# One softmax left undivided, an operand moved to ScalarE, conditioning sums kept out of one projection's end, one weight split queued behind a norm

## The chip, the cores and the metric

The kernel runs on one NeuronCore of a Trainium2 chip. A core has five engines, each working through its own list of instructions in order: TensorE (PE, matrix products), VectorE (DVE), ScalarE (ACT), GpSimd (POOL) and SyncE (SP, which here issues nearly all the DMAs). They wait for each other through semaphores. The metric is the device time of one execution in microseconds. The kernel before takes 2352.55 us, the median of three runs (2351.01 to 2356.51). A difference under about 0.2%, 4.7 us, can't be told from none.

## The reference

Two decoder layers over 256 tokens of width 2048, all in float32. Cut to what matters here:

```
c_act = silu(c)
for l in range(2):
    sh_a, sc_a, g_a, sh_m, sc_m, g_m = split(c_act @ w_ada[l] + b_ada[l])
    h = x * (1 + sc_a) + sh_a
    fq, fk, fv, ff, dq, dk, dv = split(h @ w_in[l])
    # 8 "fox" heads: a causal softmax with a decay added to the logits
    p = softmax(fq @ fk.T * 128**-0.5 + fcum_q - fcum_k)      # fcum = cumsum(log_sigmoid(ff + b_f))
    fox_o = p @ fv
    # 8 differential heads: two causal softmax maps, 64 wide each
    a = softmax(dq0 @ dk0.T / 8) - lam * softmax(dq1 @ dk1.T / 8)
    diff_o = a @ dv
    diff_o = diff_o * rsqrt(mean(diff_o**2) + 1e-5) * subln_g * (1 - lam_init)
    y = concat(fox_o, diff_o) @ w_o[l]
    x = layernorm(alpha * x + (1 + g_a) * y)
    h = x * (1 + sc_m) + sh_m
    x = layernorm(alpha * x + (1 + g_m) * (relu(h @ w_up[l])**2 @ w_down[l]))
```

## The kernel before

**Weights in two parts.** Each weight block (256 rows by 512 columns, 512 KB) is loaded by SyncE into one of seven buffers `raw`. `split_w` (L128) makes two float32r parts of it: ScalarE copies it to the high part `wh` (L135), VectorE subtracts that from it and gets the low part `wl` (L136). The activations have a high and a low part too, and each product is three matmuls: high by high, high by low, low by high (L302 to L304, and the transposed forms L328 to L331). `block` (L279) is the step that every projection loop takes: it runs what is due beside the loop, then loads and splits one block. Three blocks can be split ahead of TensorE.

**Conditioning sums beside it.** The product with `w_ada` has one row only and is done on VectorE: for each vector, 16 blocks of 512 KB are loaded (`rawa`, in the same seven buffers) and added up, scaled by one number per partition, into `acc` (the first of a sum is L147, the others L149). `side_step` (L250) takes such pieces at a rate per block, `RATES`, with one row per layer: in the mixer a rate for the first part, one for the heads, one for the output projection, then those of the MLP. If a sum is needed and not ready, `side_until` takes all its pieces at once. A finished sum is turned by eight TensorE transposes (L166) and reduced (L171, L173).

**Heads.** While the projections run, the heads are spawned as tasks whose steps come due a given number of blocks later. A differential head computes four logit tiles (two maps, two query tiles), and per map and query tile `softmax_rows` (L606): VectorE adds the mask and takes the row minimum (L612), ScalarE takes the exponential with the row sum `su` (L614), VectorE the reciprocal (L616). The second map is scaled by minus lambda over its sum (L671 on VectorE, L672 on ScalarE), and one VectorE operation divides the first map and adds the second (L674). TensorE turns the result (L622 to L624), multiplies it with the values (L681 to L683), and the output is normalized by its mean square (L687 to L692). A fox head divides its map on ScalarE (L644). Its decay comes from a matmul whose operand `FR` is one VectorE product (L877) per four heads.

**The stretch between two sub-layers.** A projection that ends a sub-layer has `proj_tail` (L349): its last blocks (four in the mixer) are all loaded first, then all their matmuls are made for query tile 0 and after that for tile 1. So tile 0 can go on while TensorE still works for tile 1: VectorE multiplies the product with the gate, adds it to the residual and takes statistics (L510 to L513), aggregates them (L517, L519), GpSimd makes one over the standard deviation (L521), and VectorE normalizes the tile in four pieces of 512 columns (L526). Tile 1 follows in the same way, piece by piece. TensorE turns the pieces (L485), ScalarE scales and shifts them by the conditioning (L498), and VectorE makes the high part of the new `hT` (L500) and the low part (L501). Then the next projection starts. There are three such stretches: after layer 0's mixer (the first norm below), after layer 0's MLP (the second) and after layer 1's mixer (the third).

**What sets the order.** The kernel is written with a layer that records the operations and lists them per engine by its own estimate of when each could run. What two operations share decides what may not be turned round; the rest can change place with any edit. `tc.issue_after(ins)` asks that the operations recorded inside it come behind `ins` on its engine.

## Time and profile before

| | |
|---|---|
| median of three runs | 2352.55 us |
| profiled execution, its own time | 2351.68 us |
| its span, first to last instruction | 2350.0 us |
| TensorE busy | 2273.3 us, 97% |
| TensorE weight loads busy | 1937.6 us, 82% |
| VectorE busy | 1801.3 us, 77% |
| ScalarE busy | 1157.2 us, 49% |
| mean granted TensorE clock | 0.995 |

The busy shares are averages over the whole span. TensorE is busy in all but a few places, so the reader looks for the places where it stood idle, and for what ended each of those waits. A timeline row gives start, duration, engine, line, operation and tiles, and in brackets the idle time of the engine just before it with what ended that time. Rows that show "x4" are several instructions of one kind merged.

### The profile page before, as it was taken

The numbers are of one execution on the slowest core, as the hardware profiler recorded it, in microseconds if no ns is written. First come the engines' busy times: TensorE is split into PE (matmuls) and PEld (weight loads), VectorE is DVE, ScalarE is ACT, GpSimd is POOL, SyncE is SP. The second block draws the span as 40 slices with busy tenths as digits, with TensorE's granted clock in tenths as the row PEclk, the third lists the DMA queues.
The fourth block names the chain that finished last, engine by engine and source line by source line (L and its number), as shares of the span: only waits on it lengthen the run. The fifth ranks groups of instructions, "written<-read, shape, count | busy, mean of one in ns | idle before, by whom it ended". The sixth has DMA issues, their size and how long they took to land.

```text
span 2350.0 us, 32557 instructions
## 1 busy us (share of the span) xinstructions
PE 2273.3 (97%) x12060; PEld 1937.6 (82%) x12060; DVE 1801.3 (77%) x2363; ACT 1157.2 (49%) x1696; POOL 35.2 (1%) x60
## 2 busy tenths in 40 slices
PE   4999999899999999999999999999999999999998
PEld 3878788699989888888877778888888888888886
DVE  7899989989888778888777976767675666555657
ACT  3543675345546346346444664544644643643542
POOL 0000010000000000000000000000000000000000
PEclk9999999999999999999999999999999999999999
DMA  9998678888898889888758877764687677755553
GB/s 346 330 331 308 207 262 311 313 314 330 302 350 300 305 281 315 314 289 302 273 185 307 295 233 242 255 212 168 225 268 241 229 244 242 228 194 190 187 190 124
DMA packets 174975, 619.32 MB, mean 264 GB/s; under 512 B 20104, under 2 KB 21208, under 8 KB 174816
## 3 DMA queue, kind: packets, MB, share of 16 engines
q1 hardware_dynamic: 174816, 617.25, 76.1%
q8 instruction: 94, 1.54, 0.3%
q14 instruction: 65, 0.53, 0.1%
HBM read 615.07 MB, written 2.10 MB: 263 GB/s over the span
## 4 chain that ended last, share of the span: by engine, by line
PE 81%; DVE 8%; DMA 5%; issue 3%; ACT 2%; POOL 0%; SPq 0%; DVEq 0%; ACTq 0%; POOLq 0%
PE mm L303 14%; PE mm L302 14%; PE mm L304 14%; PE mm L938 7%; PE bank L938 7%; PE mm L940 4%; PE bank L940 4%; PE mm L344 3%; PE mm L331 3%; PE mm L330 3%; PE mm L328 3%; DVE wl L136 3%; DMA rawa<-in_w_ada_T_dram 2%; DVE acc L149 2%; PE mm L346 2%
## 5 line engine op out<-in xcount | busy, mean ns | idle before, releaser
L135 ACT CAST wh<-raw 128x1024 fp32r<-128x1024 f32 x752 | 790.1, 1051 | 932.8 <-PE mm L304 500.1
L136 DVE TENSOR_TENSOR wl<-raw,wh 128x1024 fp32r<-128x1024 f32 x752 | 915.0, 1222 | 340.6 <-ACT wh L135 338.0
L149 DVE SCALAR_TENSOR_TENSOR acc<-rawa,cact,acc 128x1024 f32<-128x1024 f32 x368 | 471.0, 1280 | 114.2 <-DMA rawa<-in_w_ada_T_dram 57.6
L303 PE MATMUL mm<-wl,Hs 128*128 128x512 f32 x992 | 386.7, 390 | 1.5 <-DVE wl L136 1.5
L302 PE MATMUL mm<-wh,Hs 128*128 128x512 f32 x992 | 386.6, 390 | 0.0
L304 PE MATMUL mm<-wh,Hs 128*128 128x512 f32 x992 | 386.5, 390 | 0.0
L938 PE MATMUL mm<-hT,wh 128*128 128x512 f32 x768 | 286.7, 396 | 0.0
L938 PE MATMUL bank<-hT,wh 128*128 128x512 f32 x768 | 286.4, 395 | 0.0
L303 PEld LDWEIGHTS mm<-wl,Hs 128*128 128x128 f32 x992 | 186.3, 188 | 40.6 <-DVE wl L136 2.3
L304 PEld LDWEIGHTS mm<-wh,Hs 128*128 128x128 f32 x992 | 186.3, 188 | 38.8
L302 PEld LDWEIGHTS mm<-wh,Hs 128*128 128x128 f32 x992 | 186.3, 188 | 38.3
L940 PE MATMUL mm<-hT,wl 128*128 128x256 f32 x768 | 215.9, 281 | 0.0
L940 PE MATMUL bank<-hT,wl 128*128 128x256 f32 x768 | 215.8, 281 | 0.0
L302 PE MATMUL mm<-wh,hT 128*128 128x512 f32 x512 | 201.4, 400 | 5.8 <-DVE hT L500 5.7
L303 PE MATMUL mm<-wl,hT 128*128 128x512 f32 x512 | 203.2, 397 | 2.4 <-DVE wl L136 2.2
L304 PE MATMUL mm<-wh,hT 128*128 128x512 f32 x512 | 200.5, 392 | 0.0
L328 PE MATMUL mm<-hT,wh 128*128 128x256 f32 x640 | 181.2, 284 | 1.1 <-DVE hT L500 1.1
L330 PE MATMUL mm<-hT,wh 128*128 128x256 f32 x640 | 181.0, 284 | 0.2 <-DVE hT L501 0.2
L331 PE MATMUL mm<-hT,wl 128*128 128x256 f32 x640 | 180.2, 285 | 0.7 <-DVE wl L136 0.3
L938 PEld LDWEIGHTS bank<-hT,wh 128*128 128x128 f32 x768 | 144.1, 188 | 33.4
L938 PEld LDWEIGHTS mm<-hT,wh 128*128 128x128 f32 x768 | 144.1, 188 | 33.3
L940 PEld LDWEIGHTS mm<-hT,wl 128*128 128x128 f32 x768 | 145.4, 189 | 0.6 <-DVE wl L136 0.3
(256 smaller groups left out, 3000.3 us busy)
## 6 DMA issues: line engine op xcount, KB each, us to landing
rawa<-in_w_ada_T_dram SPq DMA_DIRECT2D x256, 512.0 KB, 5.3
raw<-in_w_up_dram SPq DMA_DIRECT2D x256, 512.0 KB, 4.8
raw<-in_w_down_dram SPq DMA_DIRECT2D x256, 512.0 KB, 4.6
raw<-in_w_in_dram SPq DMA_DIRECT2D x192, 512.0 KB, 5.0
rawa<-in_w_ada_G_dram SPq DMA_DIRECT2D x128, 512.0 KB, 5.2
raw<-in_w_o_dram SPq DMA_DIRECT2D x64, 512.0 KB, 4.4
gb<-in_ln_g_dram SPq DMA_DIRECT2D x12, 256.0 KB, 5.8
bb<-in_ln_b_dram SPq DMA_DIRECT2D x12, 256.0 KB, 5.3
```

The source lines that it names most:

```text
L135: nc.scalar.copy(wh, raw)
L136: nc.vector.tensor_sub(wl, raw, wh.bitcast(F32))
L149: nc.vector.scalar_tensor_tensor(acc, raw, k, acc, ALU.mult, ALU.add)
L302: nc.tensor.matmul(o, lhsT=hi, rhs=wh, start=start, stop=False)
L303: nc.tensor.matmul(o, lhsT=hi, rhs=wl, start=False, stop=False)
L304: nc.tensor.matmul(o, lhsT=lo, rhs=wh, start=False, stop=stop)
L328: nc.tensor.matmul(o, lhsT=wh[:, j, cs], rhs=hT[:, kt, 0, :], start=first and kt == kt0 and f % 2 == 0, stop=False)
L330: nc.tensor.matmul(o, lhsT=wh[:, j, cs], rhs=hT[:, kt, 1, :], start=False, stop=False)
L331: nc.tensor.matmul(o, lhsT=wl[:, j, cs], rhs=hT[:, kt, 0, :], start=False, stop=last and kt == kt1 - 1 and f % 2 == 1)
L344: nc.tensor.matmul(pu[f], lhsT=wh[:, j, cs], rhs=hT[:, kt].rearrange("p a s -> p (a s)"), start=kt == 0, stop=False)
L938: nc.tensor.matmul(pu[f], lhsT=wh[:, j, cs], rhs=hT[:, kt].rearrange("p a s -> p (a s)"), start=kt == kt0, stop=False)
L940: nc.tensor.matmul(pu[f][:, 0:S], lhsT=wl[:, j, cs], rhs=hT[:, kt, 0, :], start=False, stop=kt == kt1 - 1)
```

## The change

1. `diff_head`: all four row tiles get their exponentials first (`exp_rows`). The first map is no longer divided by its sum s0. The second map is scaled by r = -lambda s0 / s1 and added to it, in one VectorE operation per query tile. The factor s0 that the output then carries goes out in the root-mean-square normalization, whose epsilon becomes epsilon times s0 squared (`es`). A fox head takes one reciprocal for both its row tiles.
2. `fr_later`: the decay's operand `FR` is made by four ScalarE operations in place of one VectorE operation.
3. `proj_tail` gets a flag `quiet`, set in layer 0's mixer: its four blocks take no pieces of conditioning sums. Layer 0's rates rise from 0.8, 0.8, 1.0 to 0.9, 0.9, 1.12.
4. `split_w`: the first low part that is made after the first piece of a norm's tile 1 is queued behind that piece.

```diff
-RATES = ((0.8, 0.8, 1.0, 0.6, 1.2), (1.1, 0.53, 0.64, 0.25))
+RATES = ((0.9, 0.9, 1.12, 0.6, 1.2), (1.1, 0.53, 0.64, 0.25))
...
         nc.scalar.copy(wh, raw)
-        nc.vector.tensor_sub(wl, raw, wh.bitcast(F32))
+        with tc.issue_after(behind[0]) if behind else nullcontext():
+            nc.vector.tensor_sub(wl, raw, wh.bitcast(F32))
+        del behind[:]
...
-    def proj_tail(po, lhs, wrows, c0, kt0, kt1, done):
+    def proj_tail(po, lhs, wrows, c0, kt0, kt1, done, quiet=False):
...
-            ws.append(block(wrows(kb, c0), 2, CW, (room[:, i, 0], room[:, i, 1]) if i < 4 else None))
+            ws.append(block(wrows(kb, c0), 2, CW, (room[:, i, 0], room[:, i, 1]) if i < 4 else None,
+                            quiet))
...
                 for t in range(1, NT):
-                    normalize(t, q, *ms[t])
+                    ins = normalize(t, q, *ms[t])
+                    if q == 0:
+                        behind[:] = [ins]
...
-        pr = []
+        su = sm.tile([P, 2, NT], F32, tag="sd", name="su", bufs=2)
+        pr, p1 = [], []
         for qt in range(NT):
-            nk = (qt + 1) * P
-            p1, r1 = softmax_rows(pss[1][:, qt, 0:nk], qt)
-            nc.vector.tensor_mul(r1, r1, neglam[:, l:l + 1])
-            nc.scalar.mul(p1, p1, r1)
-            p0, r0 = softmax_rows(pss[0][:, qt, 0:nk], qt)
-            nc.vector.scalar_tensor_tensor(p0, p0, r0, p1, ALU.mult, ALU.add)
-            pr.append(p0)
+            for cc, p in ((1, p1), (0, pr)):
+                p.append(exp_rows(pss[cc][:, qt, 0:(qt + 1) * P], qt, su[:, cc, qt:qt + 1]))
+
+        r = sm.tile([P, NT], F32, tag="r", name="r", bufs=2)
+        nc.vector.reciprocal(r, su[:, 1, :])
+        nc.vector.scalar_tensor_tensor(r, su[:, 0, :], neglam[:, l:l + 1], r, ALU.mult, ALU.mult)
+        es = sm.tile([P, NT], F32, tag="es", name="es", bufs=4)
+        nc.vector.scalar_tensor_tensor(es, su[:, 0, :], RMS_EPS, su[:, 0, :], ALU.mult, ALU.mult)
+        for qt in range(NT):
+            nc.vector.scalar_tensor_tensor(pr[qt], p1[qt], r[:, qt:qt + 1], pr[qt], ALU.mult, ALU.add)
...
-            nc.vector.tensor_mul(FR, FG.unsqueeze(1).broadcast_to([P, 4, S]),
-                                 sel[:, g * 4:g * 4 + 4].unsqueeze(2).broadcast_to([P, 4, S]))
+            for i in range(4):
+                nc.scalar.mul(FR[:, i, :], FG, sel[:, g * 4 + i:g * 4 + i + 1])
...
-                proj_tail(pos[0], lhs_o, wo, 3 * CW, 8 - OTAIL, 8, lambda t: finish(3, pos[0], t))
+                proj_tail(pos[0], lhs_o, wo, 3 * CW, 8 - OTAIL, 8, lambda t: finish(3, pos[0], t), l == 0)
```

The edits shift the lines: L136 becomes L137, L147 and L149 become L149 and L151, L500 and L501 become L504 and L505, L510 to L519 become L514 to L523, L526 becomes L530, L612 becomes L618.

VectorE at the first norm, from tile 0's last product to tile 1's first pieces. `tmp` is the product with the gate, `mv`, `ve` and `rs` the statistics, `acc` a conditioning sum. Before:

```order
L149 SCALAR_TENSOR_TENSOR acc<-rawa,cact,acc 128x1024 x2
L510 TENSOR_TENSOR tmp<-mm,gate_2_1_3702 128x512 x2
L511 TENSOR_TENSOR xacc<-xacc,tmp 128x512 x2
L513 BN_STATS stats<-xacc 128x6 x2
L517 BN_AGGR mv<-stats 128x2
L149 SCALAR_TENSOR_TENSOR acc<-rawa,cact,acc 128x1024
L519 TENSOR_SCALAR ve<-mv 128x1
L517 BN_AGGR mv<-stats 128x2
L136 TENSOR_TENSOR wl<-raw,wh 128x1024
L526 TENSOR_SCALAR xacc<-xacc,mv,rs 128x512 x4
L519 TENSOR_SCALAR ve<-mv 128x1
L136 TENSOR_TENSOR wl<-raw,wh 128x1024
```

The same place now:

```order
L530 TENSOR_SCALAR xacc<-xacc,mv,rs 128x512 x4
L149 TENSOR_SCALAR acc<-rawa,cact 128x1024
L514 TENSOR_TENSOR tmp<-mm,gate_2_1_3497 128x512
L515 TENSOR_TENSOR xacc<-xacc,tmp 128x512
L517 BN_STATS stats<-xacc 128x6
L521 BN_AGGR mv<-stats 128x2
L523 TENSOR_SCALAR ve<-mv 128x1
L530 TENSOR_SCALAR xacc<-xacc,mv,rs 128x512 x2
L137 TENSOR_TENSOR wl<-raw,wh 128x1024
L504 CAST hT<-h_4447 128x2x256
L137 TENSOR_TENSOR wl<-raw,wh 128x1024
L505 TENSOR_TENSOR hT<-h_4447,hT 128x2x256
```

Before, tiles 0 and 1 went through the steps together, with sums and low parts between them. Now tile 0 is through all its steps first, one new sum's first piece stands ahead of tile 1, and the low parts stand behind tile 1's first two pieces, the second of them between the high and the low part of `hT`.

VectorE at the third norm, from tile 1's pieces on (`h` is ScalarE's scaled piece). Before:

```order
L526 TENSOR_SCALAR xacc<-xacc,mv,rs 128x512 x4
L500 CAST hT<-h_15312 128x2x256
L501 TENSOR_TENSOR hT<-h_15312,hT 128x2x256
L500 CAST hT<-h_15322 128x2x256
L501 TENSOR_TENSOR hT<-h_15322,hT 128x2x256
```

And now:

```order
L530 TENSOR_SCALAR xacc<-xacc,mv,rs 128x512 x3
L137 TENSOR_TENSOR wl<-raw,wh 128x1024
L504 CAST hT<-h_15116 128x2x256
L137 TENSOR_TENSOR wl<-raw,wh 128x1024
L505 TENSOR_TENSOR hT<-h_15116,hT 128x2x256
L504 CAST hT<-h_15126 128x2x256
```

Three low parts that stood ahead of tile 0's steps in the list stand behind tile 1's pieces now: the first two are in these rows, the third four pairs later.

VectorE in layer 1's first differential head, from its last logit tile to its two finished rows (`s`). Before:

```order
L616 RECIPROCAL rs<-su 128x1
L149 SCALAR_TENSOR_TENSOR acc<-rawa,cact,acc 128x1024
L674 SCALAR_TENSOR_TENSOR s<-s,rs 128x128
L616 RECIPROCAL rs<-su 128x1 x2
L561 SCALAR_TENSOR_TENSOR xacc<-bb,xacc 128x512
L671 TENSOR_TENSOR rs<-rs,neglam 128x1
L136 TENSOR_TENSOR wl<-raw,wh 128x1024
L674 SCALAR_TENSOR_TENSOR s<-s,rs 128x256
```

And now:

```order
L151 SCALAR_TENSOR_TENSOR acc<-rawa,cact,acc 128x1024
L680 RECIPROCAL r<-su 128x2
L683 SCALAR_TENSOR_TENSOR es<-su 128x2
L567 SCALAR_TENSOR_TENSOR xacc<-bb,xacc 128x512
L681 SCALAR_TENSOR_TENSOR r<-su,neglam,r 128x2
L137 TENSOR_TENSOR wl<-raw,wh 128x1024
L685 SCALAR_TENSOR_TENSOR s<-s,r 128x128
L685 SCALAR_TENSOR_TENSOR s<-s,r 128x256
```

The two finished rows now come one right behind the other, both behind the low part that stood between them.

## Rows read from the trace of the kernel before

**Rows 1.** The page's first part: busy us, share of the span, instructions.

```profile
span 2350.0 us, 32557 instructions
...
PE 2273.3 (97%) x12060; PEld 1937.6 (82%) x12060; DVE 1801.3 (77%) x2363; ACT 1157.2 (49%) x1696; POOL 35.2 (1%) x60
```

**Rows 2.** TensorE's waits: line, waited for, us in total, times, longest.

```profile
PE bank L485 <- DVE xacc L526: 15.1, 4, 6.9
...
PE mm L303 <- DVE wl L136: 4.7, 7, 1.2
...
PE bank L623 <- DVE s L674: 2.1, 4, 0.9
```

**Rows 3.** Timeline of TensorE around the first norm: start, us, operation.

```profile
443.63 0.50 PE L303 MATMUL mm<-wl,MXd 128*128 128x512 f32 x1 [1.07 <-DVE wl L136]
...
459.78 0.39 PE L304 MATMUL mm<-room,MXf 128*128 128x512 f32 x1
467.02 0.66 PE L485 MATMUL bank<-ident,xacc 128*128 128x128 f32 x2 [6.86 <-DVE xacc L526]
467.48 1.92 PE L166 MATMUL bank<-ident,acc 128*128 128x128 f32 x8
470.49 3.16 PE L485 MATMUL bank<-ident,xacc 128*128 128x128 f32 x14 [1.10 <-DVE xacc L526]
...
473.72 0.37 PE L330 MATMUL mm<-hT,wh 128*128 128x256 f32 x1
```

**Rows 4.** Timeline of VectorE before and in the first norm.

```profile
423.24 0.74 DVE L147 TENSOR_SCALAR acc<-rawa,cact 128x1024 f32<-128x1024 f32 x1
...
463.37 1.21 DVE L149 SCALAR_TENSOR_TENSOR acc<-rawa,cact,acc 128x1024 f32<-128x1024 f32 x1
...
464.74 1.16 DVE L136 TENSOR_TENSOR wl<-raw,wh 128x1024 fp32r<-128x1024 f32 x1
```

**Rows 5.** Timeline of SyncE in the first norm: the next sum's loads.

```profile
464.61 1.64 SPq L156 DMA_DIRECT2D rawa<-in_w_ada_T_dram  x2
```

**Rows 6.** Timeline around the third norm, TensorE and VectorE.

```profile
1614.59 0.69 DVE L510 TENSOR_TENSOR tmp<-mm,gate 128x512 f32<-128x512 f32 x1 [3.13 <-PE mm L304]
...
1617.88 1.92 DVE L526 TENSOR_SCALAR xacc<-xacc,mv,rs 128x512 f32<-128x512 f32 x4 [0.66 <-POOL rs L521]
...
1619.60 0.39 PE L304 MATMUL mm<-room,MXf 128*128 128x512 f32 x1
...
1620.03 0.69 DVE L510 TENSOR_TENSOR tmp<-mm,gate 128x512 f32<-128x512 f32 x1 [0.23 <-PE mm L304]
...
1623.33 1.91 DVE L526 TENSOR_SCALAR xacc<-xacc,mv,rs 128x512 f32<-128x512 f32 x4 [0.67 <-POOL rs L521]
1623.93 3.27 PEld L485 LDWEIGHTS bank<-ident,xacc 128*128 128x128 f32 x16 [3.73 <-DVE xacc L526]
...
1625.92 0.43 DVE L500 CAST hT<-h 128x512 fp32r<-128x512 f32 x1 [0.68 <-ACT h L498]
1626.38 0.69 DVE L501 TENSOR_TENSOR hT<-h,hT 128x512 fp32r<-128x512 f32 x1
...
1627.19 0.48 PE L938 MATMUL mm<-hT,wh 128*128 128x512 f32 x1
```

**Rows 7.** Windows: busy us of PE, PEld, DVE, ACT, POOL; granted clock, DMA share, GB/s.

```profile
240.00:270.00 30.00, 29.12 (x152) 21.91 (x150) 29.45 (x88) 19.33 (x43) 0.00 (x0) 1.00 0.59 193
...
443.00:460.00 17.00, 16.37 (x70) 12.99 (x70) 16.73 (x18) 4.89 (x5) 0.00 (x0) 1.00 0.96 356
...
465.00:470.00 5.00, 2.37 (x10) 2.00 (x10) 4.12 (x8) 0.00 (x0) 2.76 (x2) 0.50 0.68 211
...
1205.00:1207.00 2.00, 2.00 (x8) 1.71 (x7) 1.97 (x4) 2.00 (x5) 0.00 (x0) 0.50 0.00 0
...
1627.00:1630.00 3.00, 3.00 (x19) 2.63 (x18) 2.90 (x7) 2.53 (x6) 0.00 (x0) 0.98 0.00 0
```

**Rows 8.** DMA issues of the page's last part: count, KB each, us to landing.

```profile
rawa<-in_w_ada_T_dram SPq DMA_DIRECT2D x256, 512.0 KB, 5.3
```

More of the change, by code (lines that the diff above doesn't have):

```diff
@@ L216, in decoder @@
     hold = [0]
+    behind = []
     nop = lambda: None
@@ L525, in normalize @@
         xs = xacc[:, t, q * CW:(q + 1) * CW]
-        nc.vector.tensor_scalar(xs, xs, mean, rs, ALU.subtract, ALU.mult)
+        return nc.vector.tensor_scalar(xs, xs, mean, rs, ALU.subtract, ALU.mult).ins
     def norm_first(stats):
@@ L604, in heads_T, with exp_rows @@
         return oT
-    def softmax_rows(ps, qt):
+    def exp_rows(ps, qt, su):
         nk = (qt + 1) * P
@@ L612, in softmax_rows @@
         nc.vector.tensor_tensor_reduce(s, ps, m, 1.0, 3.0e38, ALU.add, ALU.min, mn)
-        su = sm.tile([P, 1], F32, tag="su", name="su", bufs=4)
         nc.scalar.activation(s, s, AF.Exp, bias=mn, scale=-1.0, accum_out=su)
-        rs = sm.tile([P, 1], F32, tag="rs4", name="rs", bufs=4)
-        nc.vector.reciprocal(rs, su)
-        return s, rs
+        return s
     def probs_T(p0, p1):
@@ L641, in fox_head @@
                              start=False, stop=qt == NT - 1)
+        su = sm.tile([P, NT], F32, tag="su", name="su", bufs=2)
         for qt in range(NT):
-            p, rs = softmax_rows(ps[:, qt, 0:(qt + 1) * P], qt)
-            nc.scalar.mul(p, p, rs)
-            pr.append(p)
+            pr.append(exp_rows(ps[:, qt, 0:(qt + 1) * P], qt, su[:, qt:qt + 1]))
+        rs = sm.tile([P, NT], F32, tag="rs4", name="rs", bufs=2)
+        nc.vector.reciprocal(rs, su)
+        for qt, p in enumerate(pr):
+            nc.scalar.mul(p, p, rs[:, qt:qt + 1])
         yield GAP
@@ L687, in diff_head @@
             nc.scalar.activation(o[:, qt, :], po[:, qt * P:(qt + 1) * P], AF.Square, accum_out=ms[:, qt:qt + 1])
-        nc.vector.tensor_scalar(ms, ms, 1.0 / HD, RMS_EPS, ALU.mult, ALU.add)
+        nc.vector.scalar_tensor_tensor(ms, ms, 1.0 / HD, es, ALU.mult, ALU.add)
         ri = sm.tile([P, NT], F32, tag="ri", name="ri")
```

## The prediction

> **What bounds the kernel now.** I read the page's first part first. TensorE is busy for 2273.3 of 2350.0 us, VectorE for 77% of the span [rows 1]. So a gain can only come from the 77 us in which TensorE stands idle, or from work that leaves TensorE. The second view is the table of what TensorE waited for. The largest wait that the change touches is that for the normalized residual: 15.1 us in four waits, the longest 6.9 [rows 2]. The longest is in the first norm: TensorE stops at 459.78 + 0.39 = 460.17, and I call this moment T; its pieces resume at 467.02, pause once more for 1.10 us, and the first matmul that needs the low part of the new `hT` starts at 473.72 [rows 3]. From T to there it is 13.55 us. Third I read the same stretch for VectorE: at 463.37, with tile 1 waiting, it makes a piece of a conditioning sum (1.21 us), and at 464.74 a low part (1.16 us) [rows 4]. The next sum's loads are issued there too, at 464.61 [rows 5]. The third norm shows what the stretch takes when no sums stand in it [rows 6]: its last matmul ends at 1619.60 + 0.39 = 1619.99, and the same kind of matmul starts at 1627.19, after 7.20 us.
>
> All sums are against the profiled execution's own time, 2351.68 us: 0.87 below the median of the runs shown, and inside their scatter. TensorE gates everything between these places, so I count what is taken off its idle time as taken off the whole.
>
> **First norm.** Tile 0's chain now runs alone. In the third norm it takes 5.2 us (1614.59 to 1617.88 + 1.92 = 1619.80) and is through before TensorE has finished tile 1 [rows 6]; I take the same here, so it costs nothing. Tile 1's chain by the third norm's rows: from the last matmul to the first normalized piece 1623.33 - 1619.99 = 3.34 us. Two pieces of 1.91 / 4 = 0.48 us each bring T + 4.30. The first low part, 1.16 [rows 4], ends at T + 5.46. Meanwhile the transposes start 0.12 us after the first piece (1623.93 against 1623.81), so at T + 3.94, and the scaled piece reaches the CAST 1.99 us later (1625.92), at T + 5.93; it takes 0.43, to T + 6.36. The second low part ends at T + 7.52, the low part of `hT` (0.69) at T + 8.21, and the matmul starts 0.12 later (1627.19 against 1627.07), at T + 8.33 [rows 6]. That is 13.55 - 8.33 = 5.22 us saved: **-5.2**.
>
> Ahead of tile 1 stands the first piece of the next sum, of a kind that took 0.74 us at 423.24 [rows 4]. VectorE waits there for TensorE anyway (3.13 us in the third norm [rows 6]), so the piece costs nothing if its load lands early, and 0.74 if it lands just at T. If the load lands later, everything of tile 1 is queued behind it on VectorE, and TensorE behind that. It can be issued earlier than before, because the quiet blocks leave no sum pieces to wait for, but its buffer comes free only with a low part of the tail. I take 0.74, **+0.7**, with 0 below; above see the fourth rival.
>
> The eight transposes of the old sum, 1.92 us at 467.48, ran while TensorE had nothing to do [rows 3], at half clock (0.50 over 465 to 470 [rows 7]). Now the sum ends before the tail, and they stand in running work, at full clock: half of 1.92, **+1.0** (0 to 1.9).
>
> The tail loses its sums. One wait of TensorE there, 1.07 us at 443.63 for a low part [rows 3], stood where VectorE was busy for 16.73 of 17.00 us and the DMA queues for 96% [rows 7]. With the loads and pieces gone I expect most of it to go: **-0.8** (0 to -1.1).
>
> **Sums moved forward.** The pieces don't vanish; they go into layer 0's heads and projections, at 0.9 for 0.8 per block. That is a tenth of a piece of 1.21 us [rows 4] per block, some 2.5 us of VectorE over about 21 blocks of the heads. Against it go the two products `FR` and the smaller operations of the heads. VectorE was busy for 29.45 us of the 30 from 240 to 270 [rows 7], so there it hides nothing more. I take 0, with -2.5 to +2.5 as bounds, since that is the work that may be added and what TensorE's remaining L303 waits show as losable, 4.7 - 1.07 = 3.6 us, is of the same size [rows 2, 3].
>
> **Low parts behind the piece, third and second norm.** In the third norm all three low parts were finished before. Now: pieces 1 to 3 end at 1623.33 + 3 x 0.48 = 1624.77, a low part at 1625.93, the CAST at 1626.36, the second low part at 1627.52, the low part of `hT` at 1628.21, so the matmul starts at 1628.33 and not at 1627.19 [rows 6]: +1.1. What it clears, tile 0's start, lay beneath tile 1's matmuls. In the second norm TensorE's list puts other matmuls ahead of those that need the low part; I take +0.1. Together **+1.2** (0 to 2.3).
>
> **Heads.** TensorE waited four times for finished rows `s`, 2.1 us, longest 0.9 [rows 2]. Undivided, the first map needs no reciprocal, and three of four reciprocals go, with the scaling by ScalarE. But all four exponentials are awaited before the first row, and in the first head a low part now stands before both rows. I take off two thirds: **-1.4** (0 to -2.1). `FR` on ScalarE costs nothing, since that engine is busy for 49% [rows 1]; if a head's exponential comes right behind it, its four parts delay that one by about what VectorE's product took.
>
> **Clock at the restart.** In the first norm TensorE had eight more transposes right before its matmuls. After a long idle stretch the granted clock was 0.50 (1.2 of 2.4 GHz) over 1205 to 1207, with matmuls, but 0.98 over 1627 to 1630 [rows 7]. The 2.00 us of the first stretch would be 1.0 at full clock, so a slow restart loses 1.0 and a fast one nothing. The third norm is the nearer of the two, with the same transposes ahead: **+0.3** (0 to 1.0).
> The Trainium skill (TensorE: Matmul & The Clock Gate, the part on PE-mode transpose) says that a transpose doesn't count as a busy PE in the way that a matmul does. By that rule the first matmuls behind the sixteen transposes run slow, and the term would be +1.0 in place of +0.3. The third norm's row, 0.98 with only transposes ahead of it, speaks against the rule; the row at 1205 agrees with it.
>
> **The sum.** -5.2 + 0.7 + 1.0 - 0.8 + 0 + 1.2 - 1.4 + 0.3 = -4.2; 2351.7 - 4.2 = 2347.5 us. A difference under 0.2%, 4.7 us, can't be told from none: faster means below 2347.8, slower above 2357.3. The forecast stands right at the first of these.
>
> **Rivals.**
> - *The other waits of the heads go too.* VectorE gets many short operations less, and TensorE's L303 waits for low parts (3.6 us outside the tail) vanish. For it: they stand where VectorE is full [rows 7]. Against it: the higher rates fill VectorE again. -4.2 - 3.6: 2343.9.
> - *The sums bite in layer 0.* The 2.5 us of pieces all end up in front of low parts that TensorE waits for. For it: 29.45 of 30 us busy [rows 7]. Against it: projections before and after have slack. -4.2 + 2.5: 2350.0.
> - *The fresh sum's piece is somewhat late,* so half of the first norm's gain is lost: -4.2 + 2.6, 2350.1. For it: the DMA queues are 96% busy until 460 [rows 7].
> - *Slower: the fresh sum's load is issued as late as before.* At 464.61 [rows 5] plus the 5.3 us that such a load takes at the median [rows 8] it lands at 469.9, its piece ends at 470.65, T + 10.5. Tile 1 starts only then, and the matmul comes at T + 10.5 + 8.33 = T + 18.8 and not T + 13.55: +5.3 where -4.5 was counted. The sum is -4.2 + 9.8 = +5.6, 2357.3. For it: the piece stands ahead of tile 1 in VectorE's list. Against it: the tail loads no sum pieces, so SyncE is there sooner. From a landing at about T + 4.2, 464.4, on, the change is slower than before.
> - *The change does not do what it says:* no sign of it, since the three places in the order show it; it is in none of the chances.
>
> **How the numbers follow.** Forecast 0.47; the waits gone too 0.15; sums bite 0.20; piece somewhat late 0.10; load as late as before 0.08. The forecast's own range is its sum's nearer bounds, 2345.5 to 2350. The range for 8 in 10 reaches from a part of the first rival and a little beyond for the heads' bound, 2343, to 2353, the second and third with the third norm's upper bound; it leaves out most of the fourth. Faster by over 0.2%: half of the forecast (0.26), nearly all of the first rival (0.14), and 0.05 of the second, whose bound is two-sided: 0.45. Slower by over 0.2%: the fourth rival and some chance of two mishaps together, 0.09. Within: 0.46.
>
> **What would show it.** In the profile after, the row of the first norm's wait for the residual should be about 4 us in place of 6.9 and be followed by the matmul with the low part near T + 8.3; VectorE should have no sum piece but one of 0.74 us there. The eight transposes should be in front of the tail. The wait of 1.07 us in the tail should be gone. In the third norm two low parts should stand between tile 1's pieces and the low part of `hT`, and the matmul should start 8.3 us after the last one, not 7.2. Waits for `s` should be at most 0.7 us. If VectorE waits at the fresh sum's piece for a DMA past T, the fourth rival or the third holds; if the L303 waits between 240 and 300 grow, the second does; if they vanish, the first. A gain much above 8 us, or one that comes from layer 1's projections, would prove this picture wrong.

## The result and the profile after

The changed kernel takes 2365.99 us, the median of four runs (2364.45 to 2367.14), against 2353.35 for the kernel before on the same chip. The ratio is 1.0058, with a 95% interval of 1.0045 to 1.0070: it is slower by 0.6%, where 2347.5 us and a range to 2353 were forecast. The forecast was wrong. The profiled execution took 2364.45 us.

The page's first part of the changed kernel (busy us, share of the span, instructions), to be held against [rows 1]:

```profile
span 2362.7 us, 32436 instructions
...
PE 2280.1 (97%) x12060; PEld 1941.0 (82%) x12060; DVE 1791.2 (76%) x2295; ACT 1151.5 (49%) x1680; POOL 35.3 (1%) x60
```

VectorE has 10 us less to do, and yet the span is 12.7 us longer. TensorE makes the same 12060 matmuls, but is busy 6.8 us longer: that is clock, not work (the mean granted clock is 0.992 and was 0.995). The table of what TensorE waited for (line, waited for; us, times, longest), to be held against [rows 2]:

```profile
PE bank L489 <- DVE xacc L530: 10.9, 3, 3.8
...
PE mm L306 <- DVE wl L137: 11.0, 9, 2.9
...
PE mm L334 <- DVE wl L137: 2.6, 4, 1.3
...
PE bank L625 <- DVE s L685: 1.4, 2, 1.1
```

The norms' wait fell from 15.1 to 10.9 us, and that for finished rows from 2.1 to 1.4. But the wait for low parts (L306, formerly L303) rose from 4.7 to 11.0. The timeline says where. TensorE in the first norm (start, us, operation), which answers to [rows 3]:

```profile
459.06 1.04 PE L168 MATMUL bank<-ident,acc 128*128 128x128 f32 x8
...
470.63 0.40 PE L307 MATMUL mm<-room,MXf 128*128 128x512 f32 x1
475.29 2.82 PE L489 MATMUL bank<-ident,xacc 128*128 128x128 f32 x12 [3.83 <-DVE xacc L530]
...
479.50 0.39 PE L333 MATMUL mm<-hT,wh 128*128 128x256 f32 x1 [1.00 <-DVE hT L505]
```

From the last matmul, 470.63 + 0.40 = 471.03, to the matmul that needs the low part it is 8.47 us now. So the norm itself gained 5.1 us. But it begins at 471.0 and not at 460.2: the time was lost ahead of it. TensorE's two waits in the output projection, and the granted clock behind each of them and, in the last row, at the third norm (windows: us; busy us of PE, PEld, DVE, ACT, POOL; clock, DMA share, GB/s):

```profile
423.64 0.79 PE L306 MATMUL mm<-wl,MXd 128*128 128x512 f32 x1 [2.89 <-DVE wl L137]
...
449.61 0.50 PE L306 MATMUL mm<-wl,MXd 128*128 128x512 f32 x1 [2.33 <-DVE wl L137]
```

```profile
423.60:427.00 3.40, 3.36 (x8) 2.69 (x9) 3.40 (x3) 0.00 (x0) 0.00 (x0) 0.51 0.94 284
...
451.00:454.50 3.50, 3.50 (x10) 2.71 (x9) 3.50 (x4) 1.13 (x2) 0.00 (x0) 0.52 0.87 295
...
1637.60:1642.20 4.60, 4.54 (x14) 3.86 (x15) 4.60 (x10) 1.46 (x4) 0.00 (x0) 0.50 0.50 163
```

Each of the two waits is followed by a stretch at half clock (1.2 of 2.4 GHz), so each cost about 1.7 us more here than it shows. (The Trainium skill, TensorE: Matmul & The Clock Gate, section "HAM oscillation — how this bites in real kernels", tells of a loop in which TensorE waits for a DMA in every tile, is throttled in that wait and starts the next tile slow. Here single waits for VectorE are followed by the slow clock too, but not always: after a wait of 2.56 us in one of the runs below the clock stayed at 1.00.)

The whole by stretches, from the two timelines: the last matmul of layer 0's mixer comes 10.9 us later (of which 2.9 had come about by 393 us, in the start and the heads), the norm takes 5.1 less, layer 0's MLP loses 5 between 560 and 800 us, the third norm loses 3.0, and some 1.5 are gained in between in the second norm and layer 1's heads. The 8 us of the output projection are 4.1 us more of waits (5.2 for 1.1), an estimated 3.4 of half clock and 0.8 for the transposes of one more finished sum.

### The profile page after: what moved, and what is told of

The parts are those of the page before. It is cut to its first block, busy times and chain, and to the rows that moved or that the text cites. A ratio compares the mean times of both kernels' runs of the same rounds, so it can differ in the third digit from the quotient of the medians.

```text
span 2362.7 us, 32436 instructions
## 1 busy us (share of the span) xinstructions
PE 2280.1 (97%) x12060; PEld 1941.0 (82%) x12060; DVE 1791.2 (76%) x2295; ACT 1151.5 (49%) x1680; POOL 35.3 (1%) x60
## 4 chain that ended last, share of the span: by engine, by line
PE 85%; DVE 8%; DMA 4%; issue 2%; ACT 1%; POOL 0%; SPq 0%; DVEq 0%; ACTq 0%; POOLq 0%
PE mm L306 15%; PE mm L307 14%; PE mm L305 14%; PE mm L948 8%; PE bank L948 8%; PE mm L950 4%; PE bank L950 4%; PE mm L347 4%; PE mm L334 3%; PE mm L333 3%; PE mm L331 3%; DVE wl L137 3%; DMA rawa<-in_w_ada_T_dram 2%; DVE acc L151 2%; PE mm L349 2%
## 5 line engine op out<-in xcount | busy, mean ns | idle before, releaser
L137 DVE TENSOR_TENSOR wl<-raw,wh 128x1024 fp32r<-128x1024 f32 x752 | 913.9, 1221 | 348.1 <-ACT wh L135 344.1
L151 DVE SCALAR_TENSOR_TENSOR acc<-rawa,cact,acc 128x1024 f32<-128x1024 f32 x368 | 470.8, 1279 | 113.5 <-DMA rawa<-in_w_ada_T_dram 68.2
L306 PE MATMUL mm<-wl,Hs 128*128 128x512 f32 x992 | 386.8, 390 | 1.4 <-DVE wl L137 1.4
L306 PEld LDWEIGHTS mm<-wl,Hs 128*128 128x128 f32 x992 | 186.2, 188 | 42.1 <-DVE wl L137 3.9
L306 PE MATMUL mm<-wl,hT 128*128 128x512 f32 x512 | 203.4, 397 | 4.6 <-DVE wl L137 4.4
```

The costliest lines, as they stand in the source:

```text
L137: nc.vector.tensor_sub(wl, raw, wh.bitcast(F32))
L151: nc.vector.scalar_tensor_tensor(acc, raw, k, acc, ALU.mult, ALU.add)
L306: nc.tensor.matmul(o, lhsT=hi, rhs=wl, start=False, stop=False)
```

## The experiments

All were timed in five rounds beside the kernel before, whose median lay between 2352.0 and 2353.1 us. One execution of each kernel was profiled; the readings by stretches are of that one. A *piece* is one block of `w_ada` added to a conditioning sum.

### Which part it is

The third part alone, both halves of it, the rates and the flag:

```diff
-RATES = ((0.8, 0.8, 1.0, 0.6, 1.2), ...
+RATES = ((0.9, 0.9, 1.12, 0.6, 1.2), ...
...
-                proj_tail(..., lambda t: finish(3, pos[0], t))
+                proj_tail(..., lambda t: finish(3, pos[0], t), l == 0)
```

> The kernel before with the third part of the change alone: the higher rates of layer 0 and the quiet blocks. Theory (VectorE has more work than TensorE in layer 0's output projection: 28 blocks x 1.14 us of low parts, 31 pieces x 1.19 and 11 us of gated products are 80 us against 76 us of matmuls; TensorE stalls for the difference, and its clock falls after a stall): the last matmul of layer 0's mixer ends 8 to 11 us later than before (at 468 to 471 us instead of 460.2), the norm behind it is 3 to 5 us shorter, the whole is 3 to 8 us slower than before. Rival 1 (the new order of the heads and what it shifts in the lists makes the stalls): the mixer ends within 2 us of before, the whole is 3 to 5 us faster. Rival 2 (the low parts behind the norms' pieces cost it): as rival 1.

Measured: 2367.09 us, ratio 1.0054 (1.0039 to 1.0069). The mixer's last matmul ends at 476.6 in the profiled execution (2372.55, the slowest of its runs). This part alone makes the whole loss; I had expected half of it. Not all of it arises in the same place, though: with the old heads 9.1 us are lost by 386 us, ahead of the output projection. The next run, with the same rates and heads, has lost 8.7 there; the changed kernel (2.9) and the five below that have these rates, whole pieces and the first two parts of the change have lost 2.9 to 5.7. So at these rates the first two parts take back 3 to 6 us, which a comparison at the old rates doesn't show.

The rates alone, without the flag:

> The kernel before with the higher rates of layer 0 alone, no quiet blocks. Theory: nearly the same stalls in the output projection, since the rate and not the quiet tail fills VectorE: the mixer ends 6 to 10 us later, the whole is 3 to 8 us slower. Rival 3 (it is the quiet tail, which forces the same pieces into fewer blocks): the mixer ends within 2 us of before, the whole within 2 us or faster. Rivals 1 and 2: no difference, or faster.

Measured: 2382.94 us, 1.0125 (1.0112 to 1.0138): 30 us slower, where 3 to 8 were expected. The quiet blocks win back half of what the rates lose, but hardly in the mixer, which ends at 477.8 here: the norm behind it takes 4 us longer than with them, and layer 0's MLP loses 12.6 us in place of 4.0.

The fourth part alone, and the change without the third part (`RATES` as before, no flag):

> The kernel before with the fourth part alone: the next low part behind the norm's first piece. Theory: the first norm is 1 to 3 us shorter (the sums stay in it), the third norm 3 us longer (1 us of low part, 2 us of half clock at the restart), the whole within 2 us of before. Rival 2 (this part makes most of the loss): 5 us slower or more. Rival 1: no difference.

> The changed kernel with the old rates and without the quiet blocks, so the first, second and fourth parts together. Theory: the stalls in the output projection go (the mixer ends at 458 to 461 us), the third norm's 3 us stay, the whole is within 3 us of before, some 12 us faster than the changed kernel. Rival 1: the mixer ends as late as in the changed kernel, the whole is 6 us or more slower than before. Rival 2: 5 us or more slower than before, at the norms.

Measured: 2354.85 us, 1.0004 (0.9995 to 1.0013), and 2353.42 us, 0.9998 (0.9989 to 1.0008). Both are even. So rivals 1 and 2 fall: the loss comes with the third part, the sums.

### Number or place of the pieces

My first theory, that VectorE has more work than TensorE in the output projection, was to be seen in the rates taken apart, each in the changed kernel:

```diff
-RATES = ((0.9, 0.9, 1.12, ...
+RATES = ((0.8, 0.8, 1.12, ...   # first run
+RATES = ((0.9, 0.9, 1.0, ...    # second run
```

> The changed kernel with the first two rates of layer 0 back at 0.8; only the output projection's rate stays at 1.12, with the quiet blocks. Theory (VectorE is full in the output projection: in the kernel before it is busy for 87.2 of that stretch's 87.9 us with 22 pieces, in the changed kernel the stretch has 27 pieces and takes 95.3 us): 25 or 26 pieces, the stretch takes 91 to 95 us with 3 to 6 us of waits for low parts, the whole is 5 to 12 us slower than before. Rival (the first two rates make it, by shifting the sums so that they collide): the stretch takes 89 us or less, the whole is within 3 us of before.

> The changed kernel with the output projection's rate back at 1.0, the first two rates at 0.9 and the quiet blocks kept. Theory: about 24 pieces in the output projection, 88 to 91 us; some pieces are left for the norm; the whole is 0 to 5 us slower than before. Rival (the first two rates make it): as slow as the changed kernel, 10 us or more.

Measured: 2357.14 us, 1.0019 (1.0010 to 1.0028), and 2366.86 us, 1.0054 (1.0041 to 1.0067). The theory predicted the opposite order; the rival had the right one. With the third rate back at 1.0 there are only 24 pieces in that stretch (from the projection's first matmul to the tail's), two fewer than the 26 of the kernel before, and the wait of 2.9 us at 424 is still there:

```profile
424.17 0.50 PE L306 MATMUL mm<-wl,MXd 128*128 128x512 f32 x1 [2.92 <-DVE wl L137]
```

My expectation had also misread the stretch in the kernel before: it has 26 pieces and not 22, and VectorE is busy for 80.9 us and not 87.2. The stretch as a window, before and changed (columns as above, VectorE's is the third):

```profile
360.83:448.77 87.94, 86.68 (x403) 71.30 (x401) 80.87 (x107) 40.87 (x64) 0.00 (x0) 1.00 0.87 303
...
364.56:459.85 95.29, 90.07 (x405) 73.72 (x405) 84.39 (x110) 43.34 (x66) 0.00 (x0) 0.96 0.87 314
```

So VectorE is nearly full there, but has no more work than TensorE.

The quiet blocks at the old rates:

> The changed kernel with all old rates, the quiet blocks kept: the pieces that the last four blocks took are left over and have to be made at once in the norm. Theory: the output projection as before (87 to 88 us, 22 pieces), the norm 4 to 9 us longer than the 10 us of the changed kernel without quiet blocks, the whole 3 to 8 us slower than before: the sums cost about as much in the norm as in the projection. Rival (the quiet blocks are a gain by themselves): 2 us or more faster than before.

Measured: 2354.66 us, 1.0007 (0.9998 to 1.0016): even, where 3 to 8 us were expected. The norm took 14.6 us, against 11.4 in the changed kernel with the old sums; 4 to 9 us more were expected and 3.2 came. The tail's end came no later.

VectorE's time per piece halved; the loads stay (half of each of these products is left out):

```diff
-            ada_add(acc, raw, kt, kt == 0)
+            if (l, vec) == (0, 3) and kt > 0:
+                ada_add(acc[:, 0, :], raw[:, 0, :], kt, False)
+            else:
+                ada_add(acc, raw, kt, kt == 0)
```

> The changed kernel, in which VectorE adds only the first 512 of the 1024 columns in all but the first piece of each sum for layer 0's MLP (the rest of those products is left out); all loads stay, in the same buffers. Theory (VectorE's time is what the pieces cost): a piece takes 0.65 in place of 1.27 us, 15 us less of VectorE's work in the output projection and more in the heads; the stretch before the tail falls from 95.3 to 86.5 to 89 us, its waits from 6.2 us to under 2, and the whole is 8 to 14 us faster than the changed kernel, 2352 to 2358 us. Rival (the loads of the pieces hold the buffers and the queue that the weights need): the stretch stays at 93 us or more.

> The kernel before with the same half pieces (the same products left out). Theory: it had only 1.3 us of waits in the output projection, so it gains little there; the heads and the norm gain 1 to 4 us: 2347 to 2352 us. So the changed kernel gains several times as much from it. Rival: both gain the same.

Measured: 2359.33 us, 1.0032 (1.0020 to 1.0045), and 2355.24 us, 1.0010 (1.0001 to 1.0019). Both miss what was expected. A piece fell to 0.74 us, the mixer's end came 6.5 us earlier, but the two waits stayed, at 1.13 and 1.79 us. And the kernel before got no faster from the same relief. So VectorE's time has a share in it, but not the whole.

That left the place. VectorE of the changed kernel, from the end of one sum over the second chunk's gated product (L514 to L517):

```profile
395.56 1.28 DVE L151 SCALAR_TENSOR_TENSOR acc<-rawa,cact,acc 128x1024 f32<-128x1024 f32 x1
...
401.12 1.23 DVE L137 TENSOR_TENSOR wl<-raw,wh 128x1024 fp32r<-128x1024 f32 x1 [1.42 <-ACT wh L135]
403.87 1.22 DVE L137 TENSOR_TENSOR wl<-raw,wh 128x1024 fp32r<-128x1024 f32 x1 [1.52 <-ACT wh L135]
...
409.14 0.74 DVE L149 TENSOR_SCALAR acc<-rawa,cact 128x1024 f32<-128x1024 f32 x1
...
410.40 1.27 DVE L151 SCALAR_TENSOR_TENSOR acc<-rawa,cact,acc 128x1024 f32<-128x1024 f32 x1
...
415.27 1.26 DVE L151 SCALAR_TENSOR_TENSOR acc<-rawa,cact,acc 128x1024 f32<-128x1024 f32 x1
416.46 1.21 DVE L137 TENSOR_TENSOR wl<-raw,wh 128x1024 fp32r<-128x1024 f32 x1
417.59 1.28 DVE L514 TENSOR_TENSOR tmp<-mm,gate 128x512 f32<-128x512 f32 x2
418.79 1.28 DVE L515 TENSOR_TENSOR xacc<-xacc,tmp 128x512 f32<-128x512 f32 x2
419.99 1.27 DVE L517 BATCH_NORM_STATS2 stats<-xacc 128x6 f32<-128x512 f32 x2
421.19 1.26 DVE L151 SCALAR_TENSOR_TENSOR acc<-rawa,cact,acc 128x1024 f32<-128x1024 f32 x1
422.38 1.21 DVE L137 TENSOR_TENSOR wl<-raw,wh 128x1024 fp32r<-128x1024 f32 x1
```

A sum's last piece stands at 395.56. The next sum can't start before TensorE has turned the old one, since `acc` has one buffer:

```profile
408.03 1.04 PE L168 MATMUL bank<-ident,acc 128*128 128x128 f32 x8
```

For 12.3 us VectorE makes no pieces, though their loads are in the seven shared buffers. It idles for its weights instead (1.42, 1.52). Then the four pieces that are there come with two low parts among them, and right behind them the gated product, six operations, 3.6 us. SyncE, which waits in order for a free buffer, shows what follows from it, and ScalarE the late block:

```profile
416.56 0.33 SPq L143 DMA_DIRECT2D raw<-in_w_o_dram  x1
...
422.48 0.33 SPq L143 DMA_DIRECT2D raw<-in_w_o_dram  x1
```

```profile
421.24 1.04 ACT L135 CAST wh<-raw 128x1024 fp32r<-128x1024 f32 x1 [2.02 <-DMA raw<-in_w_o_dram]
```

The load at 416.56 had waited 1.4 us for the buffer that the piece of 415.27 held, and the one at 422.48 waited 4.4 us for the piece behind the product. (In the kernel before, no load of weights waits for a piece between 396 and 420; each waits for a low part.) The block issued at 416.56 is copied at 421.24, its low part is made from 422.38 on, and TensorE, which had caught up, starts on it at 423.64. In the kernel before, the same product on VectorE:

```profile
411.23 1.28 DVE L149 SCALAR_TENSOR_TENSOR acc<-rawa,cact,acc 128x1024 f32<-128x1024 f32 x1
412.43 1.22 DVE L136 TENSOR_TENSOR wl<-raw,wh 128x1024 fp32r<-128x1024 f32 x1
413.56 1.29 DVE L510 TENSOR_TENSOR tmp<-mm,gate 128x512 f32<-128x512 f32 x2
414.76 1.29 DVE L511 TENSOR_TENSOR xacc<-xacc,tmp 128x512 f32<-128x512 f32 x2
415.96 1.28 DVE L513 BATCH_NORM_STATS2 stats<-xacc 128x6 f32<-128x512 f32 x2
417.16 2.35 DVE L136 TENSOR_TENSOR wl<-raw,wh 128x1024 fp32r<-128x1024 f32 x2
```

There the sum's end, 411.23, stood right ahead of the product, and the next sum began only at 423.24 [rows 4]. The hole between two sums covered the product, and two low parts followed it at once. The rates of 0.9 moved the sum's end four or five blocks forward (98 loads of pieces stand ahead of the projection's first weights in place of 94), and the hole away from the product. From the theory that place counts came two experiments. Fewer pieces in another place:

```diff
-RATES = ((0.8, 0.8, 1.0, ...     # in the kernel before
+RATES = ((0.7, 0.7, 1.0, ...
```

> The kernel before with its first two rates lowered from 0.8 to 0.7: 91 pieces are listed ahead of the output projection in place of 94, the projection itself has one per block as before, and the sum that ended at its block 18 ends at block 21. VectorE has less to do until then, and three pieces more in the norm. Theory of position (the hole between two sums, in which VectorE makes no pieces, covered the second chunk's gated product at 414 us): the hole comes behind that product, which now has pieces beside it, and TensorE waits 1 to 3 us there, though there are fewer pieces. Rival (only the number of pieces counts): no wait there, the mixer ends as early as before. With three pieces more in the norm the whole is 2 to 7 us slower by both, 4 or more by position.

Measured: 2372.84 us, 1.0080 (1.0065 to 1.0095). Its waits in the output projection (the kernel before has one, of 1.07 us, at the third chunk), in total and one by one:

```profile
PE mm L303 <- DVE wl L136: 3.7, 2, 2.6
```

```profile
423.88 0.50 PE L303 MATMUL mm<-wl,MXd 128*128 128x512 f32 x1 [1.13 <-DVE wl L136]
...
449.39 0.50 PE L303 MATMUL mm<-wl,MXd 128*128 128x512 f32 x1 [2.56 <-DVE wl L136]
```

At the second chunk's product the wait came as the theory of position said, at the low end. The larger one is at the third chunk's, and there the list has the changed kernel's pattern: the hole (430.0 to 438.4) ends just ahead of the product, three pieces come with only one low part, and the product follows at 443.34. With fewer pieces the mixer ends at 469.0, 8.8 us later; but 5.1 of these had come about by 395 us, before the projection, and why the heads lose them isn't shown. The whole is slower than I expected by either theory. (The profiled execution, 2364.90, was the fastest of its runs; 8 us of the median are not in it and stay unexplained.) And the same number in another place:

```diff
             final_ch = chs == (3,)
+            if l == 0 and chs == (2,):
+                hold[0] = 4      # no pieces in blocks 16 to 19
...
-                proj_tail(..., lambda t: finish(3, pos[0], t), l == 0)
+                proj_tail(..., lambda t: finish(3, pos[0], t))
```

> The changed kernel without the quiet blocks, and with four blocks (16 to 19 of the output projection) that take no piece: so the pieces of the quiet tail are moved to the second chunk's gated product's place and the other way round; the number of pieces is the same. Theory of position: the wait of 2.9 us at 424 and the half clock behind it go, the wait at 450 stays (2 us), and the pieces in the tail cost up to 2 us: the last matmul of the mixer ends 2 to 6 us earlier than the changed kernel's 471.0. Rival (the number of pieces counts): within 1.5 us of 471.

Measured: 2360.17 us, 1.0028 (1.0020 to 1.0037), 5.8 less than the changed kernel. VectorE there, from 416 us on, and TensorE's waits in the output projection:

```profile
416.68 2.34 DVE L137 TENSOR_TENSOR wl<-raw,wh 128x1024 fp32r<-128x1024 f32 x2
418.94 1.28 DVE L514 TENSOR_TENSOR tmp<-mm,gate 128x512 f32<-128x512 f32 x2
420.13 1.28 DVE L515 TENSOR_TENSOR xacc<-xacc,tmp 128x512 f32<-128x512 f32 x2
421.34 1.28 DVE L517 BATCH_NORM_STATS2 stats<-xacc 128x6 f32<-128x512 f32 x2
422.53 2.34 DVE L137 TENSOR_TENSOR wl<-raw,wh 128x1024 fp32r<-128x1024 f32 x2
```

```profile
PE mm L306 <- DVE wl L137: 0.2, 1, 0.2
```

Two low parts ahead of the product and two behind it, no piece between, and 5.2 us of waits are 0.2. The mixer ends at 462.8 and not at 471.0, more than I expected: the wait at 450, which I had thought would stay, went too; no run shows why. In all, the two kernels make the same number of pieces by the mixer's end. Nor does the number ahead of the tail order the kernels: with 25 pieces that stretch takes 85.7 us here and 91.4 in the kernel before at 0.7, with 24 it took 91.5 (third rate 1.0), with 27 it took 95.3 (the changed kernel) and with 29 it took 91.4 (first two rates 0.8). So it is shown that the place decides. That the hole is what made the old place good is read from the lists; a second buffer for `acc`, which would remove it, was not tried.

### The MLP

> The changed kernel, in which the fraction of a piece that is carried over into layer 0's MLP is set to 0.80, as it is in the kernel before (the changed kernel carries 0.76). The work and the rates are the same; some pieces of the MLP's sums fall one block earlier. Theory (what counts is where a piece falls against the loop's other VectorE work): the 4.5 us that the changed kernel loses between 560 and 800 us go, the whole is 3 to 5 us faster than the changed kernel (2361 to 2363 us). Rival (those losses are a late effect of the mixer's sums): no difference, within 1 us.

Measured: 2368.47 us, 1.0064 (1.0053 to 1.0076): no gain. But the loads still stood one block off the order of the kernel before, by rounding. So once more with 0.81:

```diff
+            rate[1] = 0.81
             side.extend([ada_G(l, 5)] + want_mod(l + 1, 0) + [ada_G(l + 1, 2)])
```

> The changed kernel with 0.81 carried into layer 0's MLP. With 0.80 (the run before) the MLP's pieces did not fall as in the kernel before: there the first pattern is a double piece every fifth block, with 0.80 the second one came a block later by rounding, as with 0.76. With 0.81 the MLP's loads stand in the same order as in the kernel before. Theory of position: the losses between 560 and 800 us (2.0, 0.8 and 2 us) go, the mixer's stay; 3.5 to 5 us faster than the changed kernel, 2361 to 2363 us. Rival: they stay, within 1 us of the changed kernel.

Measured: 2363.22 us, 1.0042 (1.0028 to 1.0057). TensorE's waits from 550 to 810 us, in the changed kernel and then in this one:

```profile
PE mm L334 <- DVE wl L137: 2.3, 3, 1.3
PE mm L331 <- ACT wh L135: 1.0, 1, 1.0
PE mm L306 <- DVE wl L137: 0.9, 2, 0.7
```

```profile
PE mm L334 <- DVE wl L137: 0.5, 2, 0.3
```

Of 4.2 us, 0.5 are left. The sums there are the same in number and rate; some pieces stand one block earlier. The median is 2.8 us lower than the changed kernel's, a little less than expected, but the two intervals overlap, and the profiled execution was the slowest of its runs; so the gain is shown in the stretch, and in the whole only by its median. A wait of 1.2 us at 1146 came back, which the kernel before has too.

### The other parts, and a version that is no slower

The fourth part only in the first norm (`if q == 0 and key == (0, 3)`), once in the changed kernel with the old sums, once by itself in the kernel before:

> The changed kernel with the old rates and no quiet blocks, and with the low part queued behind the norm's first piece in the first norm alone, not in the second and third. Theory: the third norm is back at 7.2 us and full clock, the second as before; the first keeps its gain of 2 to 3 us: 1.5 to 4 us faster than before. Rival (the queued low part gives nothing in the first norm either): within 1 us of before.

> The kernel before with only the low part queued behind the norm's first piece, in the first norm alone. Theory: the gain of 1.5 to 3 us of the kernel with the old sums is this, the first norm's 2 us: 2349.5 to 2352 us. Rival (the gain came from the undivided softmax): within 0.5 us of before.

Measured: 2350.23 us, 0.9989 (0.9980 to 0.9998), and 2352.28 us, 0.9997 (0.9988 to 1.0006). The first has the lowest median of all, 0.1% under the kernel before: its interval just leaves out 1, but the difference is below the 0.2% that can be told from none. Its third norm takes 7.15 us again. The second is even, as its rival said; but the first part alone, which the rival names, gains nothing either (next run). If the first kernel gains at all, it isn't shown by what.

The first part alone:

> The kernel before with the first part alone, the undivided first softmax. Prediction's step: 1.4 us less waiting for finished rows in layer 1, 0 in layer 0. Theory: the rows' wait falls by 0.5 to 1.5 us, and other waits of the heads take it back, since VectorE is full in layer 0's heads: within 2 us of before. Rival: 1.5 us or more faster.

Measured: 2355.25 us, 1.0013 (1.0004 to 1.0022). The wait for rows fell from 2.1 to 0.9 us, but others rose: that of the logit matmuls (L671) for a bank which ScalarE still reads to scale an earlier head's output (L702), from 0.4 to 2.3 us, and that of a new projection's first matmul (L347) from 1.2 to 2.4. The second part was not tried alone.

Two candidates that use the place of the pieces; the first is the changed kernel with rates of 0.8, 0.8 and 1.06, the fourth part in the first norm alone, and 0.80 carried over:

> A candidate: the changed kernel with the first two rates at 0.8, the third at 1.06, quiet blocks, the low part queued behind the piece in the first norm alone, and 0.80 carried into the MLP. Theory of position: the sum's end is where it was in the kernel before, so the second chunk's wait is under 0.5 us; the third chunk's is 1 to 2 us; the norm has some pieces left and takes 9 to 12 us; the whole is 0 to 4 us faster than before, no better than the kernel with the old sums (2350.2). Rival (only the number of pieces counts): 3 us or more slower than before.

> A candidate: the changed kernel with the four piece-free blocks moved from the tail to the second chunk's gated product (blocks 16 to 19), the low part queued behind the piece in the first norm alone, and 0.81 carried into the MLP. Theory of position: as the kernel with the pause (2360.2) less 4.3 us of the MLP and 1 to 2 us at the third norm: 2353 to 2355.5 us, still 0 to 2 us slower than before through the heads' 3 to 4 us. Rival (the MLP's losses stay): 2358 us or more.

Measured: 2358.37 us, 1.0030 (1.0019 to 1.0040), and 2351.39 us, 0.9995 (0.9985 to 1.0005). The first missed: it was to be 0 to 4 us faster than before and lies where the rival had it, 3 us or more slower. It waits for 2.7 us at the third chunk's product (1 to 2 were expected) and loses 4.4 us in the MLP, where 0.80 doesn't restore the order, as the run with 0.80 showed; so it doesn't decide between place and number. The second has the pause, the carried 0.81 and the fourth part in the first norm alone: 14.6 us faster than the changed kernel by three moves that take no work away, even with the kernel before, and better than the 2353 us or more that I expected.

## Why the prediction was wrong

**Sums moved forward: "I take 0, with -2.5 to +2.5".** This is the step that failed. I counted pieces and the time of each, a tenth of a piece more per block of the heads, and did not follow in the lists where they come to stand. They cost some 8 us in the output projection, two waits of 2.9 and 2.3 us with half clock behind each, and 5 us in the MLP, which I had not looked at, because neither its rate nor its pieces change. The runs showed the place in place of the number: the same pieces elsewhere take 5.2 us of waits to 0.2, and two fewer pieces than before (24 for 26) leave a wait of 2.92.

**The tail's wait, -0.8.** Wrong. It stood ahead of the tail, whose matmuls began at 448.77, behind the third chunk's product, and became 2.3 us. [Rows 7] showed VectorE full there; I read from it that taking the pieces out of the tail would help, and not that those ahead of the tail would be as much in the way.

**The first norm, -5.2 + 0.7.** Right: 13.55 us became 8.47, 5.1 less. The fresh sum's piece, 0.75 us at 470.74, cost nothing visible; the fourth rival did not happen.

**The transposes, +1.0.** Right: 1.04 us at 459.06 in the running work, 0.8 until the next matmul.

**The clock at the first norm's restart, +0.3.** Right as far as can be seen: the clock was 0.89 from 477.80 to 480.00.

**The third norm, +1.1.** The low parts' share was right. VectorE there, which answers to [rows 6]:

```profile
1635.44 0.43 DVE L504 CAST hT<-h 128x512 fp32r<-128x512 f32 x1
1635.78 1.22 DVE L137 TENSOR_TENSOR wl<-raw,wh 128x1024 fp32r<-128x1024 f32 x1
1636.92 0.69 DVE L505 TENSOR_TENSOR hT<-h,hT 128x512 fp32r<-128x512 f32 x1
```

The low part stands where it was forecast, and the stretch took 8.15 us (1629.51 to 1637.66) in place of 7.20. But the clock was 0.50 for 4.6 us behind it, some 2 us more, and the sum had no term for that: its clock term was for the first norm, and it took the third's clock as it was. It isn't the added wait by itself that did it. In the changed kernel with the old sums the same low parts make a wait of 0.71 us, and the clock is full behind it:

```profile
1627.62 0.50 PE L948 MATMUL mm<-hT,wh 128*128 128x512 f32 x1 [0.71 <-DVE hT L505]
...
1627.60:1630.60 3.00, 2.98 (x17) 2.61 (x18) 3.00 (x7) 1.24 (x3) 0.00 (x0) 1.00 0.75 246
```

With the low part moved out again the stretch is 7.15 us.

**The heads, -1.4.** Half right: the wait for rows fell by 0.7 us, and alone by 1.2, though its longest was 1.1 and not 0.7. At the old rates the heads as a whole gained nothing; at the new ones the kernel has lost 2.9 us by the output projection, where the old heads have lost 9.

**The rivals.** "The sums bite in layer 0" was the right one, and the sign named for it came: waits for low parts of 2.01 and 0.77 us between 240 and 300, where one of 0.31 had been. Its price, 2.5 us, was that of the work added and not of the waits that it causes; over the output projection VectorE was busy for 84.4 of 95.3 us, so the waits come from bursts and not from too much work in all. No rival had the slowdown in the output projection or the MLP.

## What to carry to other kernels

Where an in-order engine is nearly full (VectorE here, for 92% of the output projection), what side work costs can be decided by where each piece falls beside the loop's own bursts and not by how many there are: a change of rate shifts all later pieces, also those in stages whose rate is as before. So print the two lists around each burst, the end of a chunk above all, and look for the holes that covered it; a sum's end can be such a hole. And tune a rate only together with the place where it pauses.

## What the runs showed of the hardware

Waits of 2.2 to 2.9 us were followed by half clock for about 3.4 us in several of these kernels, and so cost more than half as much again as the table of waits shows. It was not regular. In the kept traces TensorE waited 23 times for 2.2 to 3.0 us while it was otherwise running: behind 13 of these waits the clock fell, behind 10 it stayed at 1.00. The changed kernel's wait of 2.33 us at 449.61 was followed by 0.52; the same wait, 2.33 us at 450.13, in the kernel with 0.81, which differs from it only in the MLP behind, was not:

```profile
451.00:455.00 4.00, 4.00 (x19) 3.31 (x18) 4.00 (x5) 1.37 (x2) 0.00 (x0) 1.00 0.97 301
```

Nor does the length of the wait order them: behind 2.56 us in the kernel with fewer pieces the clock stayed at 1.00.

At the third norm the same sixteen transposes were followed by 0.98 in the kernel before [rows 7], which doesn't wait behind them, by 0.50 in the changed one, which waits 0.53 us, and by 1.00 in the changed one with the old sums, which waits 0.71 us. What decides is not shown.
